# The same instructions of a two-layer encoder kernel in another order

## The chip, the cores and the metric

The kernel runs on one core of one Trainium2 chip. A core has TensorE (PE in the profile; matmuls, with the loading of weights, PEld, as work of its own), VectorE (DVE), ScalarE (ACT), GpSimd (POOL) and SyncE (SP), whose only work here is to issue transfers. The metric is the device time of one execution in microseconds, the median of a few runs.

## The reference

The reference is a trunk of two encoder layers on 256 rows of 1024 values. Layer 0 mixes tokens by RWKV-7 (a recurrence, computed here in chunks of 64 rows), layer 1 by stick-breaking attention; a quarter of the columns attends to a fixed memory. Around each mixer stand two SwiGLU feed-forwards of width 2816, and a layer norm after each step:

```python
for i in range(DEPTH):
    x = layer_norm(ALPHA * x + 0.5 * swiglu(x, ffn1_w_gate[i], ffn1_w_up[i], ffn1_w_down[i]), ln_g[i, 0], ln_b[i, 0])
    proj = x @ rwkv_w_in[j]    # layer 1: sb_w_in
    ...
    heads = jnp.concatenate([mix, memory_attention(mq, mem_k, mem_v)], axis=-1)
    x = layer_norm(ALPHA * x + heads @ w_out[i], ln_g[i, 1], ln_b[i, 1])
    x = layer_norm(ALPHA * x + 0.5 * swiglu(x, ffn2_w_gate[i], ffn2_w_up[i], ffn2_w_down[i]), ln_g[i, 2], ln_b[i, 2])
```

All of it is float32. Every weight is used once, so 301.5 MB of weights pass through the core.

## The kernel before

**Weights.** Rows stand in two halves of 128 (`hf` 0 and 1). Weights arrive in pieces of at most 128x1024 values, 512 KB. `piece()` (L824) issues the transfer into a buffer `raw` on the SP queue, has ScalarE round it to the format of the fast matmul, `hi`, and has VectorE form the remainder `lo = raw - hi`. There are 11 buffers for `raw`, 9 for `hi`, 8 for `lo`. `mm3()` (L858) multiplies with three matmuls: data high by `hi`, data high by `lo`, data low by `hi`. So TensorE's rows come in threes, such as hi_46r, lo_50r, hi_46r. A piece of a feed-forward serves four such threes, twelve matmuls, if both halves use it.

**Feed-forward.** The width of 2816 is cut into 11 blocks of 256. Each block has a gate and up piece (the accumulators ps_29r and ps_30r in PSUM), a turn of the result through TensorE (ps_5r, ps_6r), and down pieces that add into ps_25r, ps_26r, ps_27r and ps_3r. The names xTh and xTl are the turned input's high and low parts, hT_ names hold the turned hidden values.

**Mixer of layer 0.** For each half, a chain of small matmuls (64x64) with short steps of ScalarE and VectorE between (L_345r, Lm_333r, Y_340r, S_113r in the profile), with feed-forward work of the other half put between its steps where there is some.

**What sets the order.** The program doesn't issue its operations as it is written: class `Plan` (L296) records 4774 of them. `improve()` (L723) gives each a number `pri` from the table URGENCY (L139 on; the table holds differences, and their running sum is the number), and sorts by it the sequences in which loads, `hi` and `lo` are made:

```python
step = np.frombuffer(zlib.decompress(base64.b85decode(URGENCY)), "<i4")
for o, p in zip(self.ops, np.cumsum(step)):
    o.pri = float(p)
```

`order()` (L516) then takes, engine by engine, the operation that could start earliest, and among those that could start at about the same moment the one with the lowest number; it hands out the buffers of a pool as they come free. `issue()` (L762) emits the operations in that order, so all instructions have one line in the profile (L788), and each engine runs its own in just this order. Names with a number and an r are buffers, called after the first tile that had them; the same piece can have another buffer in another order.

**The end.** The last layer norm (`layer_norm`, L916, with `closing` set) is done in three parts of 512, 256 and 256 columns: statistics, the variance's scaling, a root on ScalarE, a reciprocal with one step of refinement, and for each part a subtraction with the gain and a multiplication with the bias, then three output transfers.

Of the kernel before, what the change touches and what calls it, by code (L numbers as in the profile page):

```python
# [18 lines left out]
AF = mybir.ActivationFunctionType  # L19
# [4 lines left out]
P = 128  # L24
D = 1024
# [4 lines left out]
C = 64  # L30
# [7 lines left out]
FC = 256  # L38
# [14 lines left out]
SB = dict(z0=0, z1=0, ln=2.0, e0=1.0, e1=1.5, o=10)  # L53
# [65 lines left out]
class Engine_:  # L119
# [31 lines left out]
    '$-S?;COn90zTTN%B!tEE*@mGCx6Py-Q-%?+OFcGfmi=&FT#<UKhOScfF>Vt7JV;m`;ch?MIkep?mV$W;TXj2Fe&VtGPF}{qS3c~YfoHSgWs=g-wZ'
    '^7Ro_u_=Yui{>Lx+QBWZ2u!2d+Mvn_<NP}UDFQ+#6L;Sc2y1GQ#F6OMU3l<!@70vJC%-CKB}h9-&;R*EdhJhDsTV7xbS6!aqK(seGtM-N%&;4T09'
    'oQ{K_FL?4n0&$JnBGD&$`i;|#qr?|n7;i8lO|j`v(CrVsSXeXcDSLR<B?AcpdAGZQCGfd8w+T0^h2uN%Vme$Ny0P3~>|JFKZu3D<1KJ0Gjx2bZVg'
    'A9}OGarin8BOR^PEQE5MV;nNqHH}lDuo{-b7ro&ji#{DQFdh5;7D5v>p3y%Q=H3-!Q*q^8mX6zZ(WZ7G%!2O{a<TIzJmlV_*SpY^=k(meUfT&zv-'
    ';sPI=Esr9MFemU#Vxy5T2?Z!dcj@lkmR&>@mZ>8F&j%O~ogm61zLsr}}aVT)q7b{N)H?Bd+|g2_C+HSMlU1{Cz@gf2TS3;MF}-L%4jN`oewDYhr9'
    'Gwtg^QOOM<RFB|uzW1~G8Ve|*-SXYnFnPgwQw@IJg>h-E>)T>pDZ^`42@X=^pjQ{*Egs*Y)KxZu@)^_T(N*&(&I>!G-dAuitcm7Mq9l28B**v&Q4'
    '^&pGtn{bTelbr>$BcL6`{NMqxWrnkLwL7wI<8o(xBf>9^!A>LFh`Hp*|WQTObwUwg7S-tf02_s;wubOEk^Jat7v^T{joX5;>&R;JpU<<ulm3vt^b'
    '*3w<-xEH|d{RF^-XwT&rkIkq}PPuKn-DxWQ|CXw52|T8Iw4qNh&E?>2o=QS6r_7}C4V9uV*07)$#5o-bnTrj~nQex|%1_IEM$UaF?^)b>{W*HUfD'
    'rS&z_Fnj?nv`>52Wx@GF^y~pV*vEb|JomYp?S;!?F!_k{T|=XDKN#a-d8#>5&0zWoxzB*pEIsrBeteBbDbX<<*Yg6)pGbw>xaKSSEpCz#E|#~3*3'
    'I`%2;1|fV|F#nhcDW?r{rK7h<gu+^96je<TY9?-nVv$uNd4~@AYl+DYjnn(s5smH{1WhuQ7Ip#fE&?MDg9PM(=p8jh>(C_a}ZXJc85Q_Y`jaPhaG'  # L160
    'w1=U_mg+2{jcWsQvXW>}+y_0A7-0RD6$jh*n8^;!q*VXiEt{V2%UmIv_S3aUV>}+;zSDtSGY-GhtO=<9Peq@?hZ-(_6xbz1(IjI&^X!yJQz%KezQ'
    'QzOxAQj%9o{rrTznS2w0zTRv!YKE5mxJT-^aee-4vtsBbYA<vej|TkuZQ@DM59J~?ppfypBT=l&*AgxmuQc33>W89uvk)GU%54ePFvIQWqSM#4PA'
    'qC>frdp@LCdnYg=P7++QVEd7Lq8Ovfj0OodbWdp7>=Xa7d{Y6wkT!=t_FT;=HJ&Gf5)ntdqVoUW<u9F3cX@G7p{fLqr(%k$QqQaFT)@b#1WUGM(u'
    'oULoZvud`<<F$Ax>;3XB<|3D-LW!$m+&Z0C?1CG`KRMxcIsFXIzQPHst<^xkKgs{pg8du$le8ZFT<m-G#ltU%_Z2yjYtkB5$y+Dd_^IoDp?f(l<r'
    '&p#|DQ3oE)~M=#JkGD`||d+bxwA~{}aRwLl4O5R5{%&$HV;oSS=4`&s_U1K5{UBa*3Ya;<?3JV@&Gs&lS!DzZ>=Qd-UN~eKyqI6RkDK9-a7-lHwU'
    ')uM7767KbMNS4f|=(~ouJ?WkHjr1xLY@2&K6K3w*;TxU4n65em2czzZCy>gq~bJuL)4dLbY?lD&C9Kug9yJ`}ylamMF^-ncA4CAG7<XCa-rg<CG^'
    'X)s#A+Y+FT3oB&Dq6E4taigsJ$TW>uHEDB!uqYASexoq5DW{|u(^Ia_bDEtal(tUUeTYf+p#moXYR#`@-wCvJ$za&UGT$R-m0e<?Dad%uL(n^<!}'
    'BBIiv@9>^+<x|3`m3%?}OW4NA!QuP{>S&Jdne>-K71N)0mPvmzfBzY&MC?t;Ii&c=4dg|Ip`(KPo~dV%MlEkngzq!Zs6GH0ZR_>WuF_#~|5g0DB7'
    '^B4Or^7lvdysml_6x(!tQbs*KvBp*EH$}{y<zS@W%hmCSJ+rC#U+Vgxd@P1ja0};tlzVGhE_gbOfss}6{ef$1sl_;)Rz>a3sbfF9bc|P=0uN8(@L'
    '}RBOC#G9f#b5N@EzWN2Ns9m?muwE0<n)&o56R%pB#*avCrW7oa^qA|63bp^4X1Wkr$>e#?ce)TM0&YIzujc@C~oFVgL;2qdV&GoxJ@b8r4m2Cmv$'  # L170
    '~-;+!Kf72K5)7&(l_dU<^l0IE*emHIRDXXRj)ws4iw8pRR>Z{2xdm2v1IqQz($JsC1!8bTl8(cGlUwc^Yj<|Lx49<6Le(Sb|u@Q3j>e)=**hs?*J'
    '{#i#n0&@Oll2q+08ZB?{sKPRJ5vogxsN|-sTbEfe_vd)(3-myU<WK!c+>eO;sw6DsyLg8alZ2`GE@EM-b?V|UwY{fO@Bkb<>T49n7jHU+NZ|Pno<'
    '56kobGr$-h^iWtHXe7crEA#b)NzyUdoo{C*jxZ_^kznp1bHV?(hlHcy`BmFLLG4SE=rhV1;xt)9Q!8Sk;jrS@&A7wX#M5O1ADKkl=~WEkn4@QwQ9'
    '!xgjjaRplNo$F80zsJOXM1DWjYdz`8Tz>9j>wHcZ4tt(O45c=yy|p&N{bPJ}d39>4KRVK?ChGBMGOT-jmVLgJvkLGskDu5DgPZuIlk~X>A9y7!4s'
# [1752 lines left out]
```

## Time and profile before

| | |
|---|---|
| median of 3 runs | 1057.3 us (1055.48 to 1059.38) |
| profiled execution | 1058.2 us, its span 1056.4 us |
| granted TensorE clock, mean | 0.995 |
| TensorE busy | 1041.8 us, 99% |
| VectorE busy | 886.2 us, 84% |
| ScalarE busy | 741.6 us, 70% |
| weights through the SP queue | 301.53 MB |

A busy time on TensorE runs from a matmul's start to its modelled end, and neighbours overlap: a 512-wide one shows 0.39 us, though the next starts 0.23 us after it. What TensorE waited for stands in brackets in a timeline's row, or summed in the list of waits; the chain of waits goes back from the end to whatever released each step. The prediction shows the rows.

### The profile page before, as it was taken

What the parts mean: (1) busy time and instruction counts of PE and PEld (TensorE: products, weight loads), DVE (VectorE), ACT (ScalarE), POOL (GpSimd) and SP (SyncE); (2) the same over time, 40 slices, a digit from 0 to 9 for tenths busy, and PEclk for the clock granted to TensorE, in tenths of its full rate; (3) what the DMA queues carried; (4) which work ended last, traced back from release to release, by engine and by line L of the source; (5) the groups of instructions that cost most, each with busy time, mean ns of one, the idle gap of its engine ahead of it and who ended that gap; (6) DMA issues with size and microseconds to landing.
All of it is one profiled execution on the core that took longest, in us unless ns stands there. A gap on an engine that the chain in (4) does not pass through costs nothing.

```text
span 1056.4 us, 17846 instructions
## 1 busy us (share of the span) xinstructions
PE 1041.8 (99%) x6275; PEld 835.8 (79%) x6275; DVE 886.2 (84%) x1241; ACT 741.6 (70%) x1064; POOL 5.3 (0%) x20
## 2 busy tenths in 40 slices
PE   8999999999899999999999999999999999999997
PEld 7788888877788776688888888888778777888885
DVE  6776679999799998898799765569899999976688
ACT  6665558968679877667577555457987998765573
POOL 0000000000000000000000000000000000000000
PEclk9999999999899999999999999999999999999999
DMA  9998869879399788799999976768989989998792
GB/s 307 332 368 259 265 201 357 266 247 331 130 328 336 250 273 295 247 341 315 307 325 352 311 246 208 226 213 262 369 309 315 366 274 304 366 366 256 265 317 76
DMA packets 212684, 303.19 MB, mean 287 GB/s; under 512 B 13892, under 2 KB 159728, under 8 KB 212594
## 3 DMA queue, kind: packets, MB, share of 16 engines
q1 hardware_dynamic: 212050, 301.53, 85.2%
q8 instruction: 49, 0.80, 0.3%
q10 hardware_dynamic: 544, 0.52, 0.2%
q14 instruction: 41, 0.34, 0.1%
HBM read 300.95 MB, written 1.05 MB: 286 GB/s over the span
## 4 chain that ended last, share of the span: by engine, by line
PE 95%; DMA 2%; DVE 1%; ACT 1%; issue 0%; SPq 0%; DVEq 0%; ACTq 0%
PE ps_30r L788 28%; PE ps_29r L788 27%; PE ps_26r L788 8%; PE ps_3r L788 8%; PE ps_27r L788 8%; PE ps_25r L788 8%; PE ps_5r L788 3%; PE ps_6r L788 3%; DMA raw_9r<-in_ffn_w_down_dram 1%; DMA raw_18r<-in_ffn_w_up_dram 1%; DMA raw_48r<-in_ffn_w_up_dram 1%; DMA raw_12r<-in_ffn_w_up_dram 1%; DVE x L788 0%; DVE L_345r L788 0%; DVE lo_47r L788 0%
## 5 line engine op out<-in xcount | busy, mean ns | idle before, releaser
L788 PE MATMUL ps_30r<-hi_46r,xTh 128*128 128x512 f32 (+1 forms) x70 | 28.2, 403 | 0.0
L788 PE MATMUL ps_30r<-hi_46r,xTl 128*128 128x512 f32 (+1 forms) x70 | 26.9, 385 | 0.0
L788 PE MATMUL ps_30r<-lo_17r,xTh 128*128 128x512 f32 x68 | 26.5, 390 | 0.0
L788 PE MATMUL ps_29r<-lo_11r,xTh 128*128 128x512 f32 (+1 forms) x64 | 24.6, 385 | 0.8 <-DVE lo_11r L788 0.8
L788 PE MATMUL ps_30r<-lo_11r,xTh 128*128 128x512 f32 x64 | 25.0, 390 | 0.0
L788 PE MATMUL ps_30r<-hi_10r,xTh 128*128 128x512 f32 x60 | 24.5, 409 | 0.0
L788 PE MATMUL ps_30r<-lo_8r,xTh 128*128 128x512 f32 x62 | 24.2, 391 | 0.0
L788 PE MATMUL ps_30r<-hi_10r,xTl 128*128 128x512 f32 x60 | 23.5, 392 | 0.0
L788 PE MATMUL ps_30r<-lo_14r,xTh 128*128 128x512 f32 x60 | 23.4, 390 | 0.0
L788 PE MATMUL ps_29r<-hi_65r,xTh 128*128 128x512 f32 x56 | 22.8, 407 | 0.0
L788 PE MATMUL ps_29r<-lo_17r,xTh 128*128 128x512 f32 x58 | 22.6, 390 | 0.0
L788 PE MATMUL ps_29r<-lo_47r,xTh 128*128 128x512 f32 (+1 forms) x58 | 22.2, 383 | 0.0
L788 ACT ACTIVATE idle_2r<-ps_29r 128x256 f32<-128x256 f32 (+1 forms) x27 | 11.1, 412 | 15.8 <-PE ps_29r L788 15.2
L788 PE MATMUL ps_30r<-hi_7r,xTh 128*128 128x512 f32 (+1 forms) x56 | 21.9, 392 | 0.0
L788 PE MATMUL ps_29r<-hi_65r,xTl 128*128 128x512 f32 x56 | 21.9, 392 | 0.0
L788 ACT ACT_TABLE_LOAD x16 | 20.5, 1283 | 2.0 <-issue 1.7
L788 PE MATMUL ps_30r<-lo_41r,xTh 128*128 128x512 f32 x56 | 21.9, 390 | 0.0
L788 PE MATMUL ps_29r<-lo_14r,xTh 128*128 128x512 f32 x56 | 21.8, 390 | 0.0
L788 ACT ACTIVATE idle_1r<-ps_29r 128x256 f32<-128x256 f32 (+1 forms) x27 | 11.7, 432 | 14.3 <-PE ps_29r L788 14.3
L788 PE MATMUL ps_30r<-hi_7r,xTl 128*128 128x512 f32 (+1 forms) x56 | 21.4, 383 | 0.0
L788 PE MATMUL ps_30r<-hi_65r,xTh 128*128 128x512 f32 x52 | 21.4, 412 | 0.0
L788 ACT ACTIVATE idle_2r<-ps_30r 128x256 f32<-128x256 f32 (+1 forms) x30 | 12.9, 431 | 12.0 <-PE ps_30r L788 12.0
(2124 smaller groups left out, 3945.5 us busy)
## 6 DMA issues: line engine op xcount, KB each, us to landing
raw_9r<-in_ffn_w_down_dram SPq DMA_DIRECT2D x16, 512.0 KB, 6.7
raw_48r<-in_ffn_w_down_dram SPq DMA_DIRECT2D x16, 512.0 KB, 6.0
raw_12r<-in_ffn_w_down_dram SPq DMA_DIRECT2D x16, 512.0 KB, 6.2
raw_18r<-in_ffn_w_gate_dram SPq DMA_DIRECT2D x31, 256.0 KB, 5.0
raw_18r<-in_ffn_w_up_dram SPq DMA_DIRECT2D x31, 256.0 KB, 4.6
raw_15r<-in_ffn_w_down_dram SPq DMA_DIRECT2D x15, 512.0 KB, 5.8
raw_9r<-in_ffn_w_gate_dram SPq DMA_DIRECT2D x30, 256.0 KB, 5.9
raw_9r<-in_ffn_w_up_dram SPq DMA_DIRECT2D x30, 256.0 KB, 5.8
```

The lines of the kernel that those rows point to most:

```text
L788: fn(*[at(x) for x in a], **{n: at(x) for n, x in k.items()})
```

## The change

Only the table URGENCY changes, 158 lines for 159, and with it all later line numbers by one (L788 becomes L789). The search that makes such tables was begun at the present one with another seed. The operations and the engine of each are the same; the order and the buffers differ. Of the bundles of TensorE 691 of 1612 stand at another place (27 places at most, 1.6 in the mean), of VectorE's operations 522 of 1241, of ScalarE's 462 of 1034, of SP's transfers 527 of 871, of GpSimd's none.

```diff
 PATIENCE = 8
 URGENCY = (
-    'c-l?edAN<`8#exXZJ`Vel1617LVQJ~5}C>rqRb-7EK`I`Wr$LSMCK;Slp#|pG*IS>qJdB(A{9}r`}cX?{X35L{bL_{ueF}%zOVbb&g(qSYpq4?jW'
...
+    'c-l?ecih(F8#nOtY7&w}l0pgXi1r{VQPD<QMy0e!MUkYvq?9D2rGXYvQ8bK_3N5QrNFp>;-}8BYfA{lxJ<lKa>%On`J<szvKI^!ys~W72@saEyj5'
...
 )
 SEED = 53017
```

The three places that the prediction speaks of:

The first down block of layer 0's first feed-forward, on TensorE; hi_46r and lo_50r are the block's parts before (piece raw_48r). In the present order the threes from hi_46r on directly follow the gate and up threes of hi_40r:

```order
L788 MATMUL ps_30r<-hi_40r,xTh 128x512
L788 MATMUL ps_30r<-lo_17r,xTh 128x512
L788 MATMUL ps_30r<-hi_40r,xTl 128x512
L788 MATMUL ps_26r<-hi_46r,hT_36r 128x512
L788 MATMUL ps_26r<-lo_50r,hT_36r 128x512
L788 MATMUL ps_26r<-hi_46r,hT_36r 128x512
L788 MATMUL ps_27r<-hi_46r,hT_38r 128x512
L788 MATMUL ps_27r<-lo_50r,hT_38r 128x512
```

In the new order the block has the parts hi_49r and lo_63r (piece raw_45r), and three more threes of gate and up work stand ahead of it:

```order
L789 MATMUL ps_30r<-hi_10r,xTh 128x512
L789 MATMUL ps_30r<-lo_14r,xTh 128x512
L789 MATMUL ps_30r<-hi_10r,xTl 128x512
L789 MATMUL ps_30r<-hi_13r,xTh 128x512
L789 MATMUL ps_30r<-lo_41r,xTh 128x512
L789 MATMUL ps_30r<-hi_13r,xTl 128x512
L789 MATMUL ps_30r<-hi_13r,xTh 128x512
L789 MATMUL ps_30r<-lo_41r,xTh 128x512
L789 MATMUL ps_30r<-hi_13r,xTl 128x512
L789 MATMUL ps_26r<-hi_49r,hT_36r 128x512
L789 MATMUL ps_26r<-lo_63r,hT_36r 128x512
L789 MATMUL ps_26r<-hi_49r,hT_36r 128x512
```

So TensorE reaches the block nine matmuls later (row 127 of its queue instead of row 118).

The transfers on the SP queue at the same place, before:

```order
L788 DMA raw_12r<-in_ffn_w_gate_dram 128x2x256
L788 DMA raw_12r<-in_ffn_w_up_dram 128x2x256
L788 DMA vn_314r<-in_rwkv_w_dram 1x768
L788 DMA raw_15r<-in_ffn_w_down_dram 128x1024
L788 DMA raw_18r<-in_ffn_w_gate_dram 128x2x256
L788 DMA raw_18r<-in_ffn_w_up_dram 128x2x256
L788 DMA raw_48r<-in_ffn_w_down_dram 128x1024
```

And after:

```order
L789 DMA raw_12r<-in_ffn_w_down_dram 128x1024
L789 DMA kn_313r<-in_rwkv_a_up_dram 64x768
L789 DMA vn_314r<-in_rwkv_w_dram 1x768
L789 DMA raw_15r<-in_ffn_w_down_dram 128x1024
L789 DMA raw_18r<-in_ffn_w_gate_dram 128x2x256
L789 DMA raw_18r<-in_ffn_w_up_dram 128x2x256
L789 DMA raw_48r<-in_ffn_w_gate_dram 128x2x256
L789 DMA raw_48r<-in_ffn_w_up_dram 128x2x256
L789 DMA raw_45r<-in_ffn_w_down_dram 128x1024
```

The block's piece (raw_48r before, raw_45r now, each the first down transfer behind a gate and up pair for raw_18r) has one gate and up pair more ahead of it. Some rows further, the transfers of the constants, small vectors and gup_111r, which stood behind raw_18r's down piece, now stand five pieces earlier.

Layer 1's first feed-forward near 650 us, on TensorE, before; lo_50r is the low part of one down piece:

```order
L788 MATMUL ps_29r<-hi_10r,xTh 128x512
L788 MATMUL ps_29r<-lo_11r,xTh 128x512
L788 MATMUL ps_29r<-hi_10r,xTl 128x512
L788 MATMUL ps_29r<-hi_16r,xTh 128x512
L788 MATMUL ps_29r<-lo_17r,xTh 128x512
L788 MATMUL ps_29r<-hi_16r,xTl 128x512
L788 MATMUL ps_26r<-hi_7r,hT_1042r 128x512
L788 MATMUL ps_26r<-lo_50r,hT_1042r 128x512
L788 MATMUL ps_26r<-hi_7r,hT_1042r 128x512
L788 MATMUL ps_29r<-hi_16r,xTh 128x512
L788 MATMUL ps_29r<-lo_17r,xTh 128x512
L788 MATMUL ps_29r<-hi_16r,xTl 128x512
```

After; the same down piece has the low part in lo_14r:

```order
L789 MATMUL ps_30r<-hi_7r,xTh 128x512
L789 MATMUL ps_30r<-lo_14r,xTh 128x512
L789 MATMUL ps_30r<-hi_7r,xTl 128x512
L789 MATMUL ps_29r<-hi_40r,xTh 128x512
L789 MATMUL ps_29r<-lo_44r,xTh 128x512
L789 MATMUL ps_29r<-hi_40r,xTl 128x512
L789 MATMUL ps_29r<-hi_40r,xTh 128x512
L789 MATMUL ps_29r<-lo_44r,xTh 128x512
L789 MATMUL ps_29r<-hi_40r,xTl 128x512
L789 MATMUL ps_5r<-cst,idle_2r 128x128 x2
L789 MATMUL ps_26r<-hi_46r,hT_1097r 128x512
L789 MATMUL ps_26r<-lo_14r,hT_1097r 128x512
```

The down threes of this piece (ps_26r and following) now come right after the threes that read the buffer's last content, and some forty rows earlier against the work around them. Transfer, `hi` and `lo` of the piece move ahead in their queues as well, by four places on VectorE.

The tail on VectorE, before (mv_574r holds mean and variance, raw_67r and raw_70r gain and bias):

```order
L788 BN_AGGR mv_574r<-st_573r 128x2
L788 TENSOR_SCALAR mv_574r<-mv_574r 128x1
L788 SCALAR_TENSOR_TENSOR x_79<-x_79,mv_574r,raw_67r 128x512
L788 RECIPROCAL mv_574r<-nw_288r 128x1
L788 SCALAR_TENSOR_TENSOR nw_288r<-mv_574r 128x1
L788 SCALAR_TENSOR_TENSOR mv_574r<-nw_288r,mv_574r 128x1
L788 SCALAR_TENSOR_TENSOR x_79<-x_79,mv_574r,raw_67r 128x256
L788 SCALAR_TENSOR_TENSOR x_79<-x_79,mv_574r,raw_70r 128x512
L788 SCALAR_TENSOR_TENSOR x_79<-x_79,mv_574r,raw_67r 128x256
L788 SCALAR_TENSOR_TENSOR x_79<-x_79,mv_574r,raw_70r 128x256 x2
```

After (gain and bias in raw_18r and raw_48r):

```order
L789 BN_AGGR mv_574r<-st_573r 128x2
L789 SCALAR_TENSOR_TENSOR x_79<-x_79,mv_574r,raw_18r 128x512
L789 TENSOR_SCALAR mv_574r<-mv_574r 128x1
L789 SCALAR_TENSOR_TENSOR x_79<-x_79,mv_574r,raw_18r 128x256
L789 RECIPROCAL mv_574r<-nw_288r 128x1
L789 SCALAR_TENSOR_TENSOR nw_288r<-mv_574r 128x1
L789 SCALAR_TENSOR_TENSOR mv_574r<-nw_288r,mv_574r 128x1
L789 SCALAR_TENSOR_TENSOR x_79<-x_79,mv_574r,raw_18r 128x256
L789 SCALAR_TENSOR_TENSOR x_79<-x_79,mv_574r,raw_48r 128x512
L789 SCALAR_TENSOR_TENSOR x_79<-x_79,mv_574r,raw_48r 128x256 x2
```

The 512-wide subtraction moves ahead of the variance's scaling, a 256-wide one moves between scaling and reciprocal, and the 512-wide multiplication comes one place later.

303 lines of the change are left out of this document (152 added, 151 removed).

## The prediction

> **What bounds the kernel now.** I read the page first: which engine is full, whether TensorE's clock held, and which engine carries the chain that ended last.
>
> ```profile
> span 1056.4 us, 17846 instructions
> PE 1041.8 (99%) x6275; PEld 835.8 (79%) x6275; DVE 886.2 (84%) x1241; ACT 741.6 (70%) x1064; POOL 5.3 (0%) x20
> PEclk9999999999899999999999999999999999999999
> PE 95%; DMA 2%; DVE 1%; ACT 1%; issue 0%; SPq 0%; DVEq 0%; ACTq 0%
> ```
>
> The profiled execution took 1058.2 us, 1.8 us of it outside its span of 1056.4. 95% of the chain is TensorE; the rest is DMA at the start and VectorE at the end. A busy TensorE need not be a TensorE at its pace, so the second view is the chain itself, in order of time:
>
> ```profile
> 25.88 6.30 DMA raw_18r<-in_ffn_w_up_dram
> ...
> 34.62 1.24 DVE lo_50r L788
> 35.85 0.04 issue
> 35.90 0.73 PE ps_26r L788 x2
> ...
> 300.89 4.08 PE ps_30r L788 x18
> ```
>
> Eighteen 512-wide matmuls in 4.08 us are 0.227 us each, one right behind the other. The last weight transfer on the chain ends at 32.2 us; the last wait for weights ends at 35.9 us. From there the end can come earlier only if TensorE stops less often, and later only if it stops more often. So the third view lists all waits of TensorE (us in all, times, longest):
>
> ```profile
> PE ps_6r L788 <- DVE L_345r L788: 1.8, 2, 1.2
> PE ps_3r L788 <- POOL lastc L788: 1.0, 1, 1.0
> PE ps_29r L788 <- DVE lo_11r L788: 0.8, 1, 0.8
> PE ps_5r L788 <- DVE S_113r L788: 0.6, 1, 0.6
> PE ps_5r L788 <- ACT Lm_333r L788: 0.6, 1, 0.6
> PE ps_6r L788 <- DMA x<-in_x_dram: 0.6, 1, 0.6
> PE ps_6r L788 <- ACT memKT L788: 0.5, 1, 0.5
> PE ps_26r L788 <- DVE lo_50r L788: 0.2, 1, 0.2
> PE ps_29r L788 <- DVE xTl L788: 0.2, 1, 0.2
> PE ps_29r L788 <- ACT xTh L788: 0.2, 1, 0.2
> ```
>
> They sum to 6.5 us, 0.6% of the span. That is about all an order can win, except for clock lost in a pause; the table of windows shows where that is (columns: length, then busy us of TensorE, its weight loads, VectorE, ScalarE, GpSimd, with counts; granted clock; DMA share; GB/s):
>
> ```profile
> 0.00:100.00 100.00, 97.14 (x441) 79.19 (x442) 66.90 (x75) 60.57 (x79) 1.45 (x10) 1.00 0.98 319
> 300.00:400.00 100.00, 99.97 (x708) 77.42 (x707) 96.36 (x173) 85.24 (x151) 0.95 (x2) 1.00 0.86 292
> 400.00:500.00 100.00, 99.40 (x915) 75.81 (x904) 87.04 (x119) 67.46 (x91) 0.26 (x1) 1.00 0.89 300
> 600.00:700.00 100.00, 100.00 (x453) 82.54 (x452) 57.62 (x63) 49.28 (x63) 0.00 (x0) 1.00 0.70 223
> 267.00:274.30 7.30, 5.41 (x162) 3.92 (x164) 5.94 (x11) 4.88 (x13) 0.00 (x0) 1.00 0.68 251
> 274.30:281.20 6.90, 5.61 (x126) 4.93 (x125) 3.91 (x10) 4.50 (x13) 0.67 (x3) 0.53 0.10 26
> ```
>
> In the last two rows, the RWKV chunk chain of the first half, TensorE idles 1.89 and 1.29 us, and in the second the granted clock is 0.53: 6.90 us at half speed cost some 3.4 us. The three long stretches from 300 us on hold TensorE at 99.4% or more.
>
> [...]
>
> **The change, part by part.** No operation is added, dropped or sent to another engine; the matmuls are the same in number and shape, so the 0.227 us each stay. Of 1612 bundles on TensorE 691 move, by 1.6 places in the mean; between 238 and 285 us none does.
>
> (1) The first down block. Now TensorE reaches it at 35.31 us, before VectorE has its low part:
>
> ```profile
> 33.52 1.06 ACT L788 ACTIVATE hi_46r<-raw_48r 128x1024 fp32r<-128x1024 f32 x1 [0.20 <-DMA raw_48r<-in_ffn_w_down_dram]
> 34.62 1.23 DVE L788 TENSOR_TENSOR lo_50r<-raw_48r,hi_46r 128x1024 fp32r<-128x1024 f32 x1
> 35.31 0.39 PE L788 MATMUL ps_26r<-hi_46r,hT_36r 128*128 128x512 f32 x1
> 35.90 0.50 PE L788 MATMUL ps_26r<-lo_50r,hT_36r 128*128 128x512 f32 x1 [0.20 <-DVE lo_50r L788]
> ```
>
> Start to start is 0.59 instead of 0.227 us: 0.36 us lost. In the new order nine more matmuls of gate and up work stand ahead, 9 x 0.227 = 2.04 us. On the SP queue one more 512 KB pair stands ahead of the block too: 524 KB at the 319 GB/s of the first window is 1.64 us, and ScalarE and VectorE follow the landing. The block is later by 1.64, its use by 2.04: the 0.40 us between cover the 0.36. Ends 0 and -0.36; I take -0.36, since the DMA share of 0.98 makes landing a matter of bytes alone.
>
> (2) Loads moved ahead. The constants (128x593), five small vectors and the 128x768 gate weights, 0.7 MB or 2.2 us at 319 GB/s, pass five 512 KB blocks on the SP queue, so they land 5 x 1.64 = 8.2 us earlier. Their first use, a turn of 44 columns, passes 33 rows on TensorE, 33 x 0.227 = 7.5 us: it has 0.7 us more than before. The five blocks land 2.2 us later. Each block feeds twelve matmuls, 2.72 us, and lands in 1.64, so every block behind the first down block adds 1.1 us of lead; four lie between, 4.4 us, which cover the 2.2. Without that cover TensorE would stop for up to 2.2 us; I take 0.
>
> (3) Layer 1's first feed-forward, near 650 us. One down block is used nine us earlier, its DMA, high part and low part move earlier with it, and its low part gets a buffer that was read only ten rows before. Rows that price the turnover:
>
> ```profile
> 658.48 0.39 PE L788 MATMUL ps_29r<-lo_50r,xTh 128*128 128x512 f32 x1
> 659.21 1.22 DVE L788 TENSOR_TENSOR lo_50r<-raw_42r,hi_7r 128x1024 fp32r<-128x1024 f32 x1
> 661.20 0.39 PE L788 MATMUL ps_26r<-lo_50r,hT_1042r 128*128 128x512 f32 x1
> ```
>
> Before, from the last reader's start to the next reader's start were 2.72 us. A reader holds its buffer 0.39 us, VectorE needs 1.22, and the weight load stands one matmul ahead, 0.23: with handing over (0.05 in the chain at 35.85, twice) some 1.95 us. Afterwards I count eight matmuls, one pair of turns and the high part, about 2.35 us: 0.4 us of room instead of 0.8. VectorE is 57.6% busy there; one add of 0.42 us in front of it would just use the room up. Ends 0 and +0.4; I take 0.
>
> (4) The tail. After the last matmul VectorE alone sets the end:
>
> ```profile
> 1049.97 0.15 DVE L788 TENSOR_SCALAR mv_574r<-mv_574r 128x1 f32<-128x1 f32 x1
> 1050.04 0.74 DVE L788 SCALAR_TENSOR_TENSOR x<-x,mv_574r,raw_67r 128x512 f32<-128x512 f32 x1
> 1050.16 0.20 ACT L788 ACTIVATE nw_288r<-mv_574r 128x1 f32<-128x1 f32 x1 [7.03 <-DVE mv_574r L788]
> 1051.22 0.48 DVE L788 SCALAR_TENSOR_TENSOR x<-x,mv_574r,raw_67r 128x256 f32<-128x256 f32 x1
> 1052.39 1.62 SPq L788 DMA_DIRECT2D out_dram<-x  x3
> 1052.67 0.88 DVE L788 SCALAR_TENSOR_TENSOR x<-x,mv_574r,raw_70r 128x256 f32<-128x256 f32 x2
> ```
>
> Now the 512-wide subtraction covers ScalarE's root (0.20). In the new order that subtraction runs before the variance is scaled, and a 256-wide one (0.48) covers the root: still longer than 0.20 plus the hand-over. The same operations follow in one queue, so VectorE ends at the same time; the 512-wide output, out first at 1052.39 now, is ready some 0.45 us later. Ends 0 and +0.45; the last output decides, I take +0.1.
>
> (5) Waits that no row shows. The waits of the moved places are gone with (1), but a new order can make its own. The least row for one is 0.2, the largest 1.2 us; as many as two of about 0.25 are my guess, +0.5, with ends 0 and +3.6 (three of the largest).
>
> Sum: 1058.2 - 0.36 + 0 + 0 + 0.1 + 0.5 = 1058.4 against the profiled execution, which lies 0.9 us above the median of 1057.3. Against the median: **1057.5 us**.
>
> **The rivals.** A measurement tells this kernel from no change at about 0.5%, 5.3 us: 1052.0 and 1062.6.
>
> Slower: VectorE's queue blocks between 300 and 400 us. VectorE is idle 3.64 us there, TensorE 0.03. VectorE works in order, so an add put ahead of its ScalarE copy holds up every low part behind it. Up to 3.64 us of such holding costs nothing; each us beyond is one of TensorE. For 1062.6 it takes 3.64 + 5.3 = 9 us, seven holds as long as the longest 1.2 us wait. For it speaks that 522 of VectorE's 1241 operations move; against it that before has waits on the same engine and TensorE lost 0.03. Two such us more than free would give 1059.5, seven 1064.5.
>
> Faster: the pauses of the chunk chain go. Worth 1.89 + 1.29 idle and 3.4 clock, 6.6 us: 1057.5 - 6.6 = 1051. Against it: TensorE's order there is the same bundle for bundle, and on VectorE only two pairs of neighbours swap.
>
> The clock alone changes. [...] If no window falls below, 1057.5 - 3.4 = 1054.1; if a second stretch (the same chain runs again for the second half of the rows, with the other of the two L_345r waits) halves too, 1060.9. The three times of before, 3.9 us apart, are as far apart as one such window. [...]
>
> Nothing at all: with (1) eaten by (4) and (5) the time is 1057.3, the forecast within its error.
>
> **How the numbers follow.** Forecast with "nothing", 1056 to 1059: 0.55. Clock window lost: 0.10 at 1054; a second one: 0.10 at 1061. VectorE holding: 0.19, of it 0.06 below 1062.6 and 0.13 above, up to 1066. Chain pauses gone: 0.06 at 1051. Faster by over 0.5% is the last alone, 0.06; slower 0.13; within, 0.81. The range leaves out the 0.06 below and most of the 0.13 above: 1053.0 to 1063.0. The likeliest case's own is 1056 to 1059.
>
> **What would show it.** Right: the wait for the low part at the first down block is missing and the first 100 us hold more TensorE time than 97.14; the 267 to 281 us rows come back within 0.5 us; the three stretches after 300 us stay at 99.4% or more; the last 8 us are as long to 0.5 us. Wrong in (3): a wait of TensorE on a low part near 652 us. Wrong by the VectorE rival: new waits of TensorE on low parts between 300 and 400 us, with VectorE waiting for ScalarE ahead of them. Wrong by the clock: another number of slices with a granted clock below 1.

## The result, and the profile after

| | before | after |
|---|---|---|
| median, same session | 1056.99 us (1055.48 to 1059.38, 20 runs) | 1059.46 us (1057.55 to 1063.18, 20 runs) |
| profiled execution, span | 1058.2 us, 1056.4 us | 1059.1 us, 1057.3 us |

The new order is slower by 2.5 us: the ratio is 1.0023, 95% interval 1.0015 to 1.0030. That is inside the forecast's range (1053.0 to 1063.0) and within 0.5%, but outside the likeliest case's own 1056 to 1059. The two profiled executions are only 0.9 us apart: that of before lies 1.2 us above the median of its 20 runs, that of after 0.4 below its own. So the profiles alone hide more than half of the difference.

The page of after, the lines that answer to those of before:

```profile
span 1057.3 us, 17858 instructions
PE 1042.3 (99%) x6275; PEld 834.7 (79%) x6275; DVE 885.8 (84%) x1241; ACT 742.3 (70%) x1064; POOL 5.3 (1%) x20
PEclk9999999999999999999999999999999999999998
PE 93%; DMA 4%; DVE 1%; ACT 1%; issue 0%; SPq 0%; DVEq 0%; ACTq 0%
```

TensorE has the same work and is again the bound. What changed is DMA's share of the chain that ended last, 4% for 2%. The chain itself says where (start, length, what):

```profile
33.17 6.92 DMA raw_67r<-in_ffn_w_gate_dram
40.09 0.02 issue
40.11 2.91 DMA gup_111r<-in_rwkv_g_up_dram
43.02 0.99 DVE lo_11r L789
44.01 7.85 DMA raw_18r<-in_ffn_w_down_dram
...
52.73 0.42 DVE idle_2r L789
53.15 0.04 issue
53.20 1.66 PE ps_29r L789 x6
```

Before, TensorE carries the chain from 35.9 us on. Now it takes over at 53.2, and the transfer of the gate weights (gup_111r), one of those moved ahead, stands in the chain. The waits of TensorE in the whole execution (us in all, times, longest):

```profile
PE ps_5r L789 <- ACT Y_340r L789: 1.6, 1, 1.6
PE ps_6r L789 <- DVE idle_2r L789: 1.0, 1, 1.0
PE ps_3r L789 <- POOL lastc L789: 1.0, 1, 1.0
PE ps_6r L789 <- DVE S_113r L789: 0.7, 1, 0.7
PE ps_5r L789 <- DVE L_345r L789: 0.6, 1, 0.6
PE ps_29r L789 <- DVE lo_11r L789: 0.5, 1, 0.5
PE ps_6r L789 <- ACT memKT L789: 0.5, 1, 0.5
PE ps_26r L789 <- DVE lo_63r L789: 0.4, 1, 0.4
PE ps_29r L789 <- DVE xTl L789: 0.2, 1, 0.2
```

The sum is 6.5 us, as before, so this list doesn't hold the loss: a stop of TensorE stands in it only as far as it outlasts the modelled end of the matmul before (the one at 49.8 us below, 0.49 us from start to start instead of 0.227, is not in it). The wait at the first down block, which was to go, is there (lo_63r, 0.4 for lo_50r's 0.2). The table of windows, for the stretches shown of before (columns as there):

```profile
0.00:100.00 100.00, 97.57 (x438) 79.15 (x439) 65.72 (x75) 60.03 (x77) 1.45 (x10) 1.00 0.96 317
300.00:400.00 100.00, 99.96 (x682) 77.26 (x684) 96.50 (x174) 85.37 (x151) 0.95 (x2) 1.00 0.88 293
400.00:500.00 100.00, 99.40 (x939) 75.78 (x928) 87.14 (x119) 68.05 (x90) 0.26 (x1) 1.00 0.91 301
600.00:700.00 100.00, 100.00 (x453) 82.39 (x452) 57.71 (x63) 49.43 (x63) 0.00 (x0) 1.00 0.70 222
267.00:274.30 7.30, 6.00 (x181) 4.43 (x180) 6.08 (x10) 4.70 (x9) 0.00 (x0) 1.00 0.92 344
274.30:281.20 6.90, 4.43 (x124) 3.89 (x125) 3.78 (x11) 5.64 (x16) 0.71 (x3) 0.75 0.02 4
```

The three stretches from 300 us on are as full as before. The last row has a granted clock of 0.75 instead of 0.53: the trace has 3.41 us at half clock there, that of before 6.83, so one stretch of 3.41 us (a half-speed window) fewer, which hides part of the loss in this pair of profiles. And the first row has more TensorE time (97.57 for 97.14) though that stretch does less: busy times overlap, so they are no measure of work done, and by the cut at 97 us of the table below it is 0.6 us behind. Fixed windows don't compare two orders.

So I cut both traces where both orders have finished exactly the same TensorE work, and took the time between these moments. The table has the same cuts for the kernel before written out as a fixed sequence (null) and for other experiments below; "end" is from TensorE's last matmul to the span's end. All in us:

| | to 97 | 97-238 | 238-285 | 285-402 | 402-426 | 426-609 | 609-1048 | end |
|---|---|---|---|---|---|---|---|---|
| before | 96.74 | 141.05 | 47.46 | 116.71 | 24.32 | 182.80 | 439.38 | 7.93 |
| null_before | 95.91 | 141.14 | 46.84 | 116.68 | 24.45 | 182.81 | 439.41 | 7.86 |
| h_pair (old order but for two pairs) | 95.98 | 141.10 | 46.73 | 116.71 | 24.83 | 182.78 | 439.35 | 7.92 |
| after | 97.35 | 141.20 | 47.05 | 116.76 | 24.36 | 182.86 | 439.63 | 8.09 |
| e_start (new to 97) | 98.04 | 141.08 | 45.55 | 117.14 | 24.33 | 182.78 | 439.36 | 7.91 |
| e_mid (new 97 to 515) | 96.02 | 141.15 | 47.78 | 116.68 | 25.66 | 182.77 | 439.36 | 7.88 |
| e_late2 (new from 610) | 96.07 | 141.04 | 46.50 | 116.86 | 24.72 | 182.77 | 439.61 | 8.04 |
| g_rest (new from 97) | 95.98 | 141.16 | 49.73 | 116.77 | 25.06 | 182.84 | 439.60 | 8.16 |
| f_const2 (constants back) | 96.60 | 141.17 | 47.18 | 117.40 | 25.16 | 182.87 | 439.61 | 8.12 |
| h_three (three places back) | 96.31 | 141.14 | 47.45 | 116.71 | 24.66 | 182.81 | 439.54 | 7.88 |

Against null_before, after loses 1.44 us to 97 us, 0.22 from 609 on and 0.23 at the end; the rest lies within what one order shows from profile to profile.

### The profile page after: what moved, and what is told of

Its sections match the earlier page's. It is cut to its first block, busy times and chain, and to the rows that moved or that the text cites. A ratio compares the mean times of both kernels' runs of the same rounds, so it can differ in the third digit from the quotient of the medians.

```text
span 1057.3 us, 17858 instructions
## 1 busy us (share of the span) xinstructions
PE 1042.3 (99%) x6275; PEld 834.7 (79%) x6275; DVE 885.8 (84%) x1241; ACT 742.3 (70%) x1064; POOL 5.3 (1%) x20
## 3 DMA queue, kind: packets, MB, share of 16 engines
HBM read 300.95 MB, written 1.05 MB: 286 GB/s over the span
## 4 chain that ended last, share of the span: by engine, by line
PE 93%; DMA 4%; DVE 1%; ACT 1%; issue 0%; SPq 0%; DVEq 0%; ACTq 0%
PE ps_29r L789 28%; PE ps_30r L789 27%; PE ps_3r L789 8%; PE ps_26r L789 8%; PE ps_28r L789 8%; PE ps_25r L789 8%; PE ps_5r L789 3%; PE ps_6r L789 3%; DMA raw_15r<-in_ffn_w_down_dram 1%; DMA raw_18r<-in_ffn_w_down_dram 1%; DMA raw_67r<-in_ffn_w_gate_dram 1%; DMA raw_51r<-in_ffn_w_up_dram 1%; DMA raw_48r<-in_ffn_w_up_dram 1%; DMA raw_12r<-in_ffn_w_up_dram 0%; DVE x L789 0%
## 5 line engine op out<-in xcount | busy, mean ns | idle before, releaser
L789 PE MATMUL ps_29r<-lo_14r,xTh 128*128 128x512 f32 (+1 forms) x72 | 27.6, 384 | 0.0
L789 PE MATMUL ps_29r<-lo_47r,xTh 128*128 128x512 f32 (+1 forms) x68 | 26.1, 384 | 0.0
L789 PE MATMUL ps_29r<-hi_16r,xTh 128*128 128x512 f32 (+1 forms) x62 | 25.9, 418 | 0.0
L789 PE MATMUL ps_30r<-lo_14r,xTh 128*128 128x512 f32 x66 | 25.7, 390 | 0.0
L789 ACT ACTIVATE idle_1r<-ps_29r 128x256 f32<-128x256 f32 (+1 forms) x29 | 11.6, 400 | 18.5 <-PE ps_29r L789 18.1
L789 PE MATMUL ps_30r<-lo_8r,xTh 128*128 128x512 f32 x62 | 24.2, 390 | 0.0
L789 PE MATMUL ps_29r<-lo_8r,xTh 128*128 128x512 f32 x62 | 24.2, 390 | 0.0
L789 PE MATMUL ps_29r<-hi_16r,xTl 128*128 128x512 f32 (+1 forms) x62 | 23.9, 385 | 0.0
L789 PE MATMUL ps_29r<-hi_49r,xTh 128*128 128x512 f32 x58 | 23.8, 411 | 0.0
L789 PE MATMUL ps_29r<-hi_7r,xTh 128*128 128x512 f32 x58 | 23.7, 409 | 0.0
L789 PE MATMUL ps_30r<-lo_47r,xTh 128*128 128x512 f32 x60 | 23.5, 391 | 0.1
L789 PE MATMUL ps_30r<-hi_40r,xTh 128*128 128x512 f32 (+1 forms) x60 | 23.5, 392 | 0.0
L789 PE MATMUL ps_30r<-hi_62r,xTh 128*128 128x512 f32 x58 | 23.4, 403 | 0.0
L789 PE MATMUL ps_30r<-lo_63r,xTh 128*128 128x512 f32 x60 | 23.4, 390 | 0.0
L789 ACT ACTIVATE idle_2r<-ps_30r 128x256 f32<-128x256 f32 (+1 forms) x27 | 10.8, 399 | 17.9 <-PE ps_30r L789 17.9
L789 PE MATMUL ps_30r<-hi_40r,xTl 128*128 128x512 f32 (+1 forms) x60 | 23.0, 384 | 0.0
L789 PE MATMUL ps_29r<-hi_7r,xTl 128*128 128x512 f32 x58 | 22.8, 393 | 0.2 <-DVE xTl L789 0.2
L789 PE MATMUL ps_29r<-hi_49r,xTl 128*128 128x512 f32 x58 | 22.7, 392 | 0.0
L789 PE MATMUL ps_30r<-hi_62r,xTl 128*128 128x512 f32 x58 | 22.7, 391 | 0.0
L789 ACT ACTIVATE idle_2r<-ps_29r 128x256 f32<-128x256 f32 (+1 forms) x28 | 12.4, 442 | 14.3 <-PE ps_29r L789 14.3
L789 PE MATMUL ps_30r<-hi_13r,xTh 128*128 128x512 f32 (+1 forms) x56 | 22.2, 396 | 0.0
L789 PE MATMUL ps_30r<-hi_7r,xTh 128*128 128x512 f32 x54 | 22.1, 409 | 0.0
```

The source lines that it names most:

```text
L789: fn(*[at(x) for x in a], **{n: at(x) for n, x in k.items()})
```

## The experiments

Each kernel holds the same instructions as both orders. e_mid and g_rest mix the two tables; all others replace the table by a fixed list, in which `order()` may only take the head of each engine's list:

```diff
-URGENCY = (
+SEQUENCE = (
...
+                    if self.queue and (at[e] >= len(self.queue[e]) or o.i != self.queue[e][at[e]]):
+                        continue
...
+            self.queue = {e: [x // 8 for x in seq if x % 8 == n] for n, e in enumerate(("PE", "DVE", "ACT", "POOL", "SP"))}
+            place = {x // 8: k for k, x in enumerate(seq)}
+            self.groups = {k: sorted(g, key=place.get) for k, g in self.groups.items()}
```

**What the comparison can tell.** The kernel before, its order kept, written as such a list:

```diff
-    'c-l?edAN<`8#exXZJ`Vel1617LVQJ~5}C>rqRb-7EK`I`Wr$LSMCK;Slp#|pG*IS>qJdB(A{9}r`}cX?{X35L{bL_{ueF}%zOVbb&g(qSYpq4?jW'
+    'c-nQGd%TWiy2s!5dEa$#D3OS<$sy;Rl2S3`FiH$55s8!%86s(vG-Nbnh?K|>i
...
```

> The old order itself, given as a written sequence instead of a table of priorities: the same instructions in the same order and buffers. What its ratio differs from 1 is the error of such a comparison: 1.000 within 0.0008, or the other runs' small differences mean less than their intervals say. Its profile gives the old order's start and middle once more: no wait at the first down block, or one of up to 0.4 us.

1056.90 us (12 runs), 1057.29 for the kernel before; ratio 0.9996 (0.9988 to 1.0005). A tenth of a per cent, about 1 us, is what these intervals can carry. A ratio is the record's estimate from the runs of both kernels and not the quotient of the two medians given; the quotients would be 1.0008 for e_start, 1.0016 for e_mid and 0.9995 for h_pair below, all within the intervals.

**Which part of the program pays.** The new order in one stretch, the old one in the others. Only the list or the table differs; here its first line in e_start, in e_mid and in e_late:

```diff
+SEQUENCE = (
+    'c-nQGdAQGI`p3WPImePcVhoAMa#ds~3@M|;XcLi0nM6jBh@`QMBEyh~43UVGW
...
+URGENCY = (
+    'c-l?edEAZF7dG&HOi4)69F?I6Q54D$LI?>V5|PXqieD(nkRc+W$dF_T86r|qB
...
+SEQUENCE = (
+    'c-nQGdA!bL`p2K`oMS8NSjvPlwhU<$N`y0tjHN^*vSiDUl17=zGDJp^vSf%vW
...
```

> The new order in the first 97 us alone, the old order behind it (105 of TensorE's bundles stand at another place than before). Theory S, the loss arises in the start, where weights arrive barely in time: the two profiles stand 1.07 us further apart at 68 us than at 31 us, and the medians differ by 2.5 us, so 1058.1 to 1059.5. Theory L, the loss is spread over all moved places: 105 of 691 moved bundles, 0.4 us of the 2.5, 1057.4. Theory C, the clock stretch of the RWKV chunk chain near 270 us: 1057.0.

> The new order from 97 to about 515 us alone, the old order before and behind. Theory S: 1057.0 as before. Theory L: 180 of 691 moved bundles, 0.65 us, 1057.6. Theory C: the chunk chain and its clock lie in this stretch, 1059.5.

> The new order from about 515 us to the end alone, with the tail's moved subtraction. Theory S: 1057.0, and 1057.1 with the tail's 0.1. Theory L: 398 of 691 moved bundles, 1.4 us, 1058.4. Theory C: 1057.0.

e_start 1058.09 (11 runs), ratio 1.0013 (1.0004 to 1.0021). e_mid 1058.93 (11), 1.0010 (1.0001 to 1.0019). e_late 1059.52 (11), 1.0019 (1.0010 to 1.0027), all against 1057.22. But e_late's seam at 515 us made a wait that neither order has:

```profile
PE ps_3r L747 <- ACT hT_1042r L747: 1.0, 1, 1.0
```

In its trace the stretch 426 to 609 takes 184.20 us, 1.3 more than in any other profile. The stretch 285 to 402 takes 118.8, 2.1 more than in null_before, though the order there is the old one: ScalarE was late behind a transfer that took 7.3 us to land, and TensorE waited 1.0 and 0.5 us. So one execution can hold waits that others of the same order don't have, and e_late says nothing on the new order. I cut again, at 610 us (e_late2), and tried everything but the start (g_rest); their tables begin

```diff
+SEQUENCE = (
+    'c-nQGdAyHh`p3W9ImcF(PPPmxLu8buEG30ALdH@e5>XKuQpzZ!EThOMr7RhuA
...
+URGENCY = (
+    'c-l?edEAZF7dG&HjHQyKB#{garW7G#DWp(_sLYxS$(T@-B(q2q5}9Ral2V3W%
...
```

> The new order from about 610 us to the end alone, cut where both orders have done the same work on all engines (the earlier cut near 515 us made a wait of its own, 1.0 us on hT_1042r). If the profiles of the stretch are right: between 610 and 1048 us the new order loses 0.25 us, and the tail 0.1: 1057.6. If the late part carries the 2.0 us which the earlier run showed: 1059.2.

> The old order in the first 97 us, the new order everywhere behind it (the mirror of the run with the new start alone). If the start costs the 1.3 us by which the three profiles with the new start stand behind the three with the old one at 97 us: 2.4 less 1.3 over the old kernel, 1058.3. If the start is not the cause: 1059.5 as the new kernel.

e_late2 1057.22 (12 runs), ratio 1.0004 (0.9993 to 1.0015); g_rest 1058.65 (11), 1.0019 (1.0010 to 1.0028), against 1057.30. So the start costs 1.4 us (0.4 to 2.2), the part from 97 to 515 about 1 us (0.1 to 2.0), the part from 610 on nothing that can be told from zero. Start and rest (1.4 + 2.0) exceed the whole 2.5 by less than their intervals, and how the loss divides between the start and the middle is known no better than these intervals say.

**The start: the constants, or the first down block?** From 20 to 60 us null_before's chain is TensorE alone, without a wait:

```profile
31.74 3.40 PE ps_30r L747 x15
35.14 0.68 PE ps_26r L747 x3
```

So the old order normally has no wait at the first down block; the 0.36 us that the prediction counted on were of that one execution. (The seven other profiles with the old start have none either.) In after, VectorE and ScalarE show what holds TensorE at 50 and at 53 us:

```profile
48.98 1.22 DVE L789 TENSOR_TENSOR lo_47r<-raw_9r,hi_40r 128x1024 fp32r<-128x1024 f32 x1
50.35 1.23 DVE L789 TENSOR_TENSOR lo_17r<-raw_12r,hi_16r 128x1024 fp32r<-128x1024 f32 x1 [0.15 <-ACT hi_16r L789]
51.59 1.22 DVE L789 TENSOR_TENSOR lo_14r<-raw_15r,hi_43r 128x1024 fp32r<-128x1024 f32 x1
52.73 0.41 DVE L789 TENSOR_TENSOR idle_2r<-idle_2r,ps_29r 128x256 f32<-128x256 f32 x1
```

```profile
46.42 1.06 ACT L789 ACTIVATE hi_62r<-raw_70r 128x1024 fp32r<-128x1024 f32 x1 [2.79 <-DMA raw_70r<-in_ffn_w_up_dram]
50.49 1.06 ACT L789 ACTIVATE hi_43r<-raw_15r 128x1024 fp32r<-128x1024 f32 x1 [0.17 <-DMA raw_15r<-in_ffn_w_down_dram]
51.46 0.36 ACT L789 ACTIVATE idle_2r<-ps_29r 128x256 f32<-128x256 f32 x1
```

```profile
49.76 0.39 PE L789 MATMUL ps_30r<-hi_40r,xTh 128*128 128x512 f32 x1
50.25 0.50 PE L789 MATMUL ps_30r<-lo_47r,xTh 128*128 128x512 f32 x1
...
52.66 0.39 PE L789 MATMUL ps_30r<-hi_10r,xTl 128*128 128x512 f32 x1
53.20 0.50 PE L789 MATMUL ps_29r<-hi_62r,xTh 128*128 128x512 f32 x1
```

ScalarE waits 2.79 us for raw_70r, the first piece behind the moved loads. From there ScalarE and VectorE run piece after piece close behind the landings. The two stops have different reasons. At 49.76 us TensorE wants lo_47r, the low part of raw_9r, the second piece behind the moved loads, and VectorE ends it at 50.20: the piece is late for its own use, and start to start is 0.49 us instead of 0.227. At 52.66 us TensorE wants ps_29r, which an add on VectorE frees at 53.14. The add needs a ScalarE step first and stands in VectorE's queue behind lo_14r; both are queued behind pieces that TensorE doesn't need yet. Start to start is 0.54 us. The moved loads are small, but each takes a place on the SP queue:

```profile
35.20 0.34 SPq L789 DMA_DIRECT2D cst<-in_const_dram  x1
35.97 0.31 SPq L789 DMA_DIRECT2D idle_2r<-in_rwkv_mu_dram  x1
36.65 0.28 SPq L789 DMA_DIRECT2D idle_2r<-in_rwkv_a_dram  x1
37.93 0.26 SPq L789 DMA_DIRECT2D idle_2r<-in_rwkv_k_k_dram  x1
...
40.11 0.36 SPq L789 DMA_DIRECT2D gup_111r<-in_rwkv_g_up_dram  x1
40.80 0.40 SPq L789 DMA_DIRECT2D raw_70r<-in_ffn_w_gate_dram  x1
```

The seven issues ahead of raw_70r's take 5.6 us (35.20 to 40.80), where 0.7 MB at the 319 GB/s of the prediction would be 2.2. The trace's semaphores tell what they waited for: in 861 of 863 cases a transfer of the SP queue uses the semaphore of the one issued eight places earlier, and each issue from 33.17 to 41.49 us starts 16 to 64 ns after that earlier transfer has landed. So this program has at most eight transfers under way, and a load of 3 KB holds one of the eight places like one of 256 KB. With the small loads in the places little is left to move: from 38 to 42 us the DMA engines moved 172 GB/s in after (busy share 0.55), 349 in null_before (1.10). That is 0.7 MB less, by my estimate another 2.0 us at 349 GB/s, on top of the 2.2 for the loads' own bytes. In null_before the dip comes later and is shallower (211 GB/s from 46 to 48 us), and no wait of TensorE in the chain to 60 us follows from it.

To undo this one part, the transfers and the small operations on them were put back, in the rest of the new order. The run's program has them behind four of the five pieces that they had passed, not behind all five, as the expectations of this run and the next say; raw_18r's down piece still comes after them:

```diff
 DMA raw_67r<-in_ffn_w_up_dram
-DMA cst<-in_const_dram
-DMA idle_2r<-in_rwkv_mu_dram
...
-DMA gup_111r<-in_rwkv_g_up_dram
 DMA raw_70r<-in_ffn_w_gate_dram
...
 DMA raw_15r<-in_ffn_w_down_dram
+DMA cst<-in_const_dram
+DMA idle_2r<-in_rwkv_mu_dram
...
+DMA gup_111r<-in_rwkv_g_up_dram
 DMA raw_18r<-in_ffn_w_down_dram
```

> The new order everywhere, but the loads of the constants, the five small vectors and the gate weights, with their turn on TensorE and the four small operations of ScalarE and VectorE that read it, put back behind the five weight blocks that they had passed. Theory S with the constants as its cause: the TensorE waits at 50.2 us (0.38) and 53.2 us (0.31) go, the one at 37.65 us (0.36) stays; 0.7 to 1.5 us under the new kernel, 1058.0 to 1058.8. Theory S with the first down block as its cause: 1059.5 as the new kernel. Theories L and C: 1059.5.

f_const: 1059.87 (9 runs), ratio 1.0023 (1.0013 to 1.0033). It didn't come back, but by my own doing: the vectors' small operations now stood on VectorE ahead of an add that TensorE needs, and waited for their late transfer:

```profile
PE ps_29r L747 <- DVE idle_1r L747: 1.1, 1, 1.1
```

f_const2 has them behind both adds:

```diff
-TENSOR_SCALAR vc<-vc 128x20
-TENSOR_TENSOR rkb<-cst,vc 128x72
-TENSOR_SCALAR vc<-vc 128x6
 TENSOR_TENSOR idle_1r<-idle_1r,ps_29r 128x256
 TENSOR_TENSOR lo_41r<-raw_18r,hi_7r 128x1024
 TENSOR_TENSOR idle_2r<-idle_2r,ps_30r 128x256
+TENSOR_SCALAR vc<-vc 128x20
+TENSOR_TENSOR rkb<-cst,vc 128x72
+TENSOR_SCALAR vc<-vc 128x6
```

> The new order with the constants' loads put back behind the five weight blocks as in the run before, but now VectorE's three small operations on them stand behind the two adds of the hidden values, which had waited behind them (TensorE lost 1.21 us at 51.85 us there). If the loads that pass the weight blocks cause the start's loss: that wait and those at 50.2 and 53.2 us go, 0.7 to 1.2 us less than the new kernel, 1058.3 to 1058.8. If only the first down block does: 1059.5.

1058.94 (11 runs), ratio 1.0016 (1.0007 to 1.0024). In its trace the stops near 50 and 53 us are gone, and TensorE's order to 97 us takes 96.60 us instead of 97.35 and 98.04. A stop of 0.38 us at the first down block remains there; f_const and h_three, with the same order at that place, don't have it. The excess of all 512-wide matmuls between 14 and 98 us over 0.2267 us each sums it up: null_before 1.25, after 2.89, e_start 3.1, f_const2 1.98, h_three 1.48 us. In after 1.39 of the 1.64 more are three stops with the slower matmul behind each: 0.61 at the first down block, 0.37 at 49.8 and 0.41 at 52.7. By this trace the moved loads cost about 0.8 us and the first down block's place about 0.6. The first is the firmer: the stops near 50 and 53 us stand in both profiles with the loads moved ahead and in none with the old order or in f_const2 and h_three. The stop at the first down block comes and goes with one and the same order there (0.51, 0.42 and 0.38 us in after, e_start and f_const2, none in f_const and h_three). The ratios alone (1.0023 against 1.0016) don't separate either from nothing.

**The chunk chain near 273 us.** On VectorE two pairs of neighbours swap. The old order with only these swapped:

```diff
-TENSOR_TENSOR L_345r<-L_345r,ps_6r 64x6x64
 TENSOR_TENSOR L_345r<-L_345r,ps_5r 64x6x64
+TENSOR_TENSOR L_345r<-L_345r,ps_6r 64x6x64
...
-TENSOR_TENSOR S_113r<-S_113r,ps_6r 128x192
 TENSOR_TENSOR S_113r<-S_113r,ps_5r 128x192
+TENSOR_TENSOR S_113r<-S_113r,ps_6r 128x192
```

> The old order with only two pairs of neighbours on VectorE swapped as in the new order: the two L_345r updates of the chunk chain near 273 us, and the two scalings behind them. If the swapped pair makes the longer pauses there: TensorE's gap ahead of the L_345r matmuls is 1.81 us instead of 1.43 and the next one 1.24 instead of 0.95 to 1.06, as in all five profiles with the new order there; 0.6 us over the old kernel, 1057.9, give or take the 0.9 that 11 runs can tell. If it is something else of the new order: 1.43 and 1057.3.

1056.84 (11 runs), ratio 0.9989 (0.9981 to 0.9998). The waits did move, as in after:

```profile
PE ps_5r L747 <- ACT Y_340r L747: 1.6, 1, 1.6
PE ps_6r L747 <- DVE idle_2r L747: 1.0, 1, 1.0
```

A shorter time with longer pauses called for a repeat:

> The run with the two swapped pairs once more, on whatever chip it falls to. Its profile had the longer pauses (1.80 and 1.24 us) but no slice at half clock, and its time was 0.11% under the old kernel (0.02 to 0.19). If that was a gain: under 1.000 again, 1056.3 to 1057.0. If the pauses cost what they are longer: 1057.9. If it was chance: 1.000 within 0.0008.

1057.41 (11 runs), ratio 1.0001 (0.9993 to 1.0010). The swap lengthens two pauses, by about 0.4 and 0.2 us, and the time doesn't show it; the stage 238 to 285 takes 46.73 and 47.12 in these two, 46.84 in null_before. The other way to arrange the same updates puts both ahead of a reduction that holds them up:

```diff
-TENSOR_REDUCE rs_606r<-ps_27r 128x2
-TENSOR_TENSOR L_345r<-L_345r,ps_6r 64x6x64
 TENSOR_TENSOR L_345r<-L_345r,ps_5r 64x6x64
+TENSOR_TENSOR L_345r<-L_345r,ps_6r 64x6x64
+TENSOR_REDUCE rs_606r<-ps_27r 128x2
```

> The old order with the two L_345r updates swapped and both moved ahead of the reduction rs_606r, so that VectorE reads one bank while ScalarE copies the other, and each then takes the other's. If the loss of the swapped pair comes from VectorE being late by the reduction (0.68 us): the gap of 1.43 us shrinks to 1.1 to 1.3, 0.1 to 0.3 us under the old kernel, 1057.1. If the swap alone costs: 1.8.

1058.19 (11 runs), ratio 1.0008 (0.9999 to 1.0017): the first pause didn't shrink and the one for idle_2r grew to 1.7. No gain there.

**All three repairs together:** f_const2 with the two pairs back as well, and the old order of VectorE in the end. The end's part:

```diff
 BN_AGGR mv_574r<-st_573r 128x2
+TENSOR_SCALAR mv_574r<-mv_574r 128x1
 SCALAR_TENSOR_TENSOR x_79<-x_79,mv_574r,raw_18r 128x512
-TENSOR_SCALAR mv_574r<-mv_574r 128x1
-SCALAR_TENSOR_TENSOR x_79<-x_79,mv_574r,raw_18r 128x256
 RECIPROCAL mv_574r<-nw_288r 128x1
...
```

> The new order with three places as in the old one: the constants' loads (as in the second run on them), the two pairs of neighbours near 273 us, and VectorE's order in the tail. If these are the named causes: 1.1 and 0.6 and 0.16 less than the new kernel's 1059.5, 1057.6; what is left over the old kernel would be the pauses without a releaser between 402 and 426 us and 0.2 us of small gaps behind 609 us. If the causes lie elsewhere: 1059.5.

1058.64 (11 runs), ratio 1.0007 (0.9999 to 1.0016). In its trace the last stage is 7.88 us again (8.04 to 8.16 in all profiles with the new end), and TensorE alone carries the chain through the start:

```profile
49.31 2.72 PE ps_30r L747 x12
52.03 0.19 PE ps_6r L747
52.21 1.58 PE ps_29r L747 x6
```

About two thirds of the loss is back by the ratio (1.0023 to 1.0007), with intervals that overlap by 0.0001. The times don't tell which of the three places gave it back; by h_pair the two pairs had nothing to give. No order here beats the kernel before in a repeated run.

**What stays open: 97 to 515 us.** e_mid and g_rest are slower, yet their stages agree with the old order's except 238 to 285 and 402 to 426. In the first, g_rest has three half-speed windows where null_before has one (mean granted clock 0.86 and 0.95 over 250 to 285 us). e_mid has one as well (0.95); its 0.94 us more are a pause of 0.88 us ahead of 258.48 us, inside the small matmuls of the chunk chain, for which the trace names no releaser. In the second, eight profiles with the old order have 24.32 to 24.83, six with the new one 24.36 to 25.66. The extra is a pause of the same kind, in e_mid

```profile
418.66 0.27 PE L783 MATMUL ps_3r<-vn_314r,Sk_344r 64*64 64x64 f32 x2 [0.67 <-issue]
```

and in f_const at another place:

```profile
406.20 0.27 PE L747 MATMUL ps_3r<-Tt_332r,Lm_333r 64*64 64x64 f32 x2 [0.95 <-issue]
```

Over both stages there are six such pauses of 0.3 us or more, in four of the six profiles with the new order from 97 us on and in none of the eight with the old one. after's own profile has none (24.36), and why the new order should have them oftener I don't know. They don't fall just anywhere, though. Counted from TensorE's first matmul as 0, they stand ahead of matmul 1492 (in e_mid and g_rest), 2890 (f_const and g_rest), 3018 (f_const2) and 3144 (e_mid), that is 11, 12 and 13 times about 127.1 matmuls behind the first. This is a length that the kernel's own `order()` reckons with: FETCH = 5500.0 ns and CHUNK = 127.1 matmuls (L132 and L133 of the kernel before), with a stall wherever TensorE would pass two such places in less than that time. The last section says what arrives there. These are the program's own numbers: no run here changed them or shows that limit of 5.5 us, so the cause stays argued. The 0.2 us from 609 on appear in every profile with the new late order, spread over many places without a wait; no cause was found.

## Why the prediction was right or wrong

- **The sum.** Forecast about no change (1057.5), measured 2.5 us more. The side and the range held; the likeliest case was too low by 2 us, since steps (1) and (2) took a gain and a zero where there were two losses. The range is 10 us wide, four times the change, so that it held says little for the mechanism, and what step (5) added for waits of no known place stood in for losses that steps (1) and (2) had denied: that is luck.
- **Step (1), the wait at the first down block goes, -0.36: wrong.** Its row was one execution's. null_before has no wait there; after loses 0.51, e_start 0.42 and f_const2 0.38, and the two others with the new order there nothing. TensorE reached the block 1.9 us later (34.98 in null_before, 36.91 in after), about as counted. The landing came later by more than the bytes: ScalarE starts on the piece at 32.4 us in null_before, at 35.3 in after, 2.9 us for the 1.64 of one more pair (1.8 against the profiled execution of before, whose piece was itself late, at 33.52). "The DMA share of 0.98 makes landing a matter of bytes alone" was the sentence that failed: with a share of 1.04 the DMA engines moved 221 GB/s from 26 to 28 us in after, and 373 in null_before with 1.05, so the share doesn't fix the rate. That the first 100 us hold more TensorE time than 97.14 came true (97.57) and proves nothing, as the table by stages shows.
- **Step (2), the moved loads are covered by 4.4 us of lead: wrong, about 0.8 us.** The price failed first: the seven loads took 5.6 us of places in the queue, not the 2.2 of their bytes, and from 38 to 42 us the DMA engines stood half idle (busy share 0.55). So the lead did not cover the second piece's own use (0.37 us lost at 49.8). And it was counted for the pieces alone: at 52.7 us TensorE stopped for an add that stood, in order, behind a piece it didn't need (0.41).
- **The VectorE rival** had an order on VectorE as the cause, but with an add that holds up low parts, and between 300 and 400 us, where TensorE lost 0.04 (99.96). At 53 us it was the other way round, a low part that held up an add, and cost some 0.4. I had looked for it where VectorE has the least idle time, not where the pieces arrive just in time.
- **Step (3), buffer turnover near 650 us, 0: right.** No wait of TensorE on a low part stands there; the window 600 to 700 holds 100.00.
- **Step (4), the tail, +0.1: right in mechanism, measured +0.19** (8.09 us in the mean of six profiles with the new end, 7.90 in the mean of seven with the old one), and gone when VectorE's old order is put back. The rows of after:

```profile
1050.45 0.24 DVE L789 BATCH_NORM_AGGREGATE mv_574r<-st_573r 128x2 f32<-128x18 f32 x1
1052.76 1.53 DVE L789 SCALAR_TENSOR_TENSOR x<-x,mv_574r,raw_48r 128x512 f32<-128x512 f32 x3
1053.53 1.30 SPq L789 DMA_DIRECT2D out_dram<-x  x3
```

  From the aggregate's start VectorE needs 3.84 us, as before (1049.70 to 53.55, 3.85); the first output is issued 3.08 us after it instead of 2.69.
- **Step (5), waits no row shows, +0.5 (0 to +3.6): about right in size** for the part behind 97 us, some 1 us, but they are pauses without a releaser, not the waits meant. The kernel's own `order()` has a term for pauses at such places, which the step left unread.
- **The rows from 267 to 281 us come back within 0.5 us: wrong for the pauses, right for the time.** They grew (longest 1.6 for 1.2, with another releaser), through the two swapped pairs that I took for nothing; together the two windows' idle time is 3.77 us for 3.18. h_pair and its repeat show no cost in time.
- **The clock rival: right that windows come and go, not as this change's doing.** Over 250 to 285 us the mean granted clock is 0.90 in before, 0.95 in most profiles, 1.00 in e_start, 0.86 in g_rest: none to three half-speed windows of 3.41 us. before, null_before and e_start have the same order there and two, one and none; their stage 238 to 285 takes 47.46, 46.84 and 45.55 us, so the two windows of before cost about 1.9 us, not the 3.4 that the prediction gave them. The two windows that I took for the kernel's normal state were one more than usual, part of why that execution was slow. No run here shows what starts a window: with one and the same order there the number differed from execution to execution.

## What to carry to other kernels

Compare two orders between moments at which both have finished the same work, and with a repeat of the old one: a wait of 0.4 us in one profile need not be the kernel's, and a fixed window counts waiting matmuls as busy (here 97.57 us for 97.14 with less done). When loads are moved ahead on an in-order queue, price the places they take (here 5.6 us) and not their bytes alone (2.2 us), and follow what stands behind the delayed pieces on each engine: the first operation that the bound engine needs pays, be it a piece itself (0.37 us here) or an add queued behind one (0.41). In a kernel whose bound engine is 99% busy, a search's other result can move some 40% of the bound engine's bundles and change 0.2%; only some ten runs a side and a null experiment make that readable.

## What the hardware showed unexpectedly

- Five loads of 3 to 10 KB were issued 0.7 to 1.3 us apart on the SP queue, no closer than the 256 KB transfer behind them (40.11 and 40.80): with eight transfers under way at most, each waited for an earlier one to land and was issued 16 to 64 ns after that landing. They are not free for being small.
- Instruction fetches are transfers, too, one queue of their own in the list of DMA queues (packets, MB, share of time):

```profile
q8 instruction: 49, 0.80, 0.3%
```

  In six pauses of TensorE without a releaser, TensorE resumed 1.2 to 1.5 us after one of these packets had landed (404.8 to 406.20 in f_const, 417.2 to 418.66 in e_mid). They come every 3 to 8 us among the small matmuls and mostly every 10 to 34 us elsewhere, 49 for 6275 matmuls, one per 128; the pauses stand 127.1 matmuls or a multiple apart. Over all 14 profiles TensorE passes no place of this spacing, 672 in all, less than 1.0 us after the packet landed. In the six pauses the packet landed 4.7 to 5.8 us after TensorE had passed the place before; at these four places the old order's profiles have 1.5 to 4.8. That TensorE waited for its instructions fits all of this and is likely; no experiment tested it.
- The number of half-speed windows in the chunk chain changes between none and three (mean granted clock over 250 to 285 us 1.00 to 0.86), and between none and two with the order there unchanged (1.00 to 0.90).
